# A hybrid decoder layer on one core: normalization in place, other buffers and another engine order at the four entries into a gated product

## The chip, the cores and the metric

The kernel runs on one core of a Trainium2 chip. The metric is the device time of one execution in microseconds, as the median of several runs. The engines are TensorE (PE; PEld is its weight load), VectorE (DVE), ScalarE (ACT), GpSimd (POOL) and SyncE (SP), whose queue issues most of the DMAs.

## The reference

One layer on x of 1024 tokens by 1024 features, all in fp32:

```python
x = x + 0.5 * swiglu(rms_norm(x, ffn1_norm), w_gate, w_up, w_down)       # D_FF = 2816
h = rms_norm(x, mix_norm)
fq, fk, fv, f_logit, sq, sk, sv, g_fox, g_sb = split_columns(h @ w_in)
...                                                                       # two attentions, 8 heads of 64 each
merged = sigmoid(g_fox) * (y_fox @ w_branch_fox) + sigmoid(g_sb) * (y_sb @ w_branch_sb)
x = x + merged @ w_out
x = x + 0.5 * swiglu(rms_norm(x, ffn2_norm), w_gate2, w_up2, w_down2)
x = x + sigmoid(rms_norm(x, ple_norm) @ w_ple_gate) * (p @ w_ple_proj)
```

`rms_norm` divides each token by the root of its mean square over the features and multiplies by a gain for each feature.

## The kernel before

x lies transposed: features on the 128 partitions, tokens along the row. `X[half]` holds 8 slices k of 128 features for one half of 512 tokens. Every fp32 operand is split in two parts that TensorE takes at its fast rate, a high part (a cast on ACT) and a low part (the fp32 value minus the high one); a product of two operands is three products, high by high, high by low and low by high. A "product" below is 12 matmuls of 128x128 by 128x512: four k and three combinations. An operand's split is `prep` for weights (`split`, L104 to L106, cast L105, subtraction L106) and `high` and `low` (L550 to L554) for activations.

The large matrix products use a block scheme with 7 products of sums and differences of blocks in place of 8. The activations of a gated product (`make_up`) are four quadrants (half of the tokens by half of the features) and the combinations that the scheme needs: `B[1]` and `B[2]` are half 0 (k 0 to 3 and 4 to 7), `B["12"]` and `B[3]` the same of half 1, `B[5]`, `B[6]`, `B[7]` and `B[4]` sums and differences. The weights' blocks are loaded by `load(n)` (two DMAs of 512 KB on SP's queue), summed by `sums(n)` and split by `prep(n, m)`; `product(n, m)` multiplies block m of column group n. The down products (`make_down`) work the same way, in chunks of 7 products, i from 0 to 6, each of four groups t of 12 matmuls (48 in all), with an eviction into X after each group (L442, L440).

There are four entries into a gated product: at the start (`first_entry`, ffn1), after ffn1's down pass (`mix_start`, the 6 column groups of the two mixer gates), after the output projection (`second_entry`, ffn2), and after ffn2's down pass (`ple_start`, 4 column groups). At an entry the half 0 of X is finished first, then half 1. For each half:

- `norm_sq` squares a slice on ACT (L189) and adds it up on GpSimd or VectorE (L191); `norm_sum` sums over the partitions with four tiny matmuls against a column of ones (L199), adds epsilon on VectorE (L201) and takes the power -0.5 on GpSimd (L202); `norm_row` transposes this into a row in PSUM, the same on all partitions (L208).
- `norm_mul` multiplies slice, gain and row on VectorE (L212) into slots of their own; `norm_high` and `norm_low` split half 0 into `B[1]` and `B[2]` (L217, L221); `combo_a` and `combo_b` do this for half 1 into `B["12"]` and `B[3]`.
- `plain(f, half)` is the direct product of column group 0 (f says which of its two blocks of 128 columns), 24 matmuls each (L482), whose result goes through the activation on ACT (`silu`, L490).
- `combo_t`, `combo_l`, `combo_u`, `combo_v`, `combo_s`, `combo_d` and `combo_e` make `B[5]`, `B[6]`, `B[7]` and `B[4]`. `combo_t` subtracts the high part of a quadrant of half 0 and then its low part (L590, L591), `combo_u` works on GpSimd (L598), `combo_v` on VectorE (L601), and `combo_d` subtracts and adds the two parts of `B[2]` (L611, L612).

At the mix, second and last entry this runs inside the last chunk of the down product before it: `up_begin` and `up_step` are called for each product i and group t, then `up_first` and `products`. After these comes the list of `up_order`, in which the product s is followed by its eviction, `begin(s)` and the preparation of product s + 4. At the start `first_entry` writes the order out by hand; there `busy` gives TensorE eight products of a zero tile with the slices of x as these arrive (L232).

Inside these parts each engine runs its instructions in the order in which the program issues them (`manual_schedule`), so an instruction that waits holds up all that are behind it on its engine. Buffers come from pools by tag (`BUFS`): a new tile of a tag waits until an older one of the same tag has been read for the last time.

In the last entry `finish` multiplies the gate with the projected embedding (`pd`), adds the residual (`xe`) and stores the result; for the groups n of 0 to 2 it does this on GpSimd (L1553, L1554), for n of 3 on VectorE, and `fetch` loads the two for later blocks.

Of the kernel before, what the change touches and what calls it, by code (L numbers as in the profile page):

```python
# [36 lines left out]
def tile_hybrid_decoder_layer(  # L37
# [131 lines left out]

    def norm_begin(X, i, tags):  # L170

        return {"x": X, "g": gains[:, i, :], "tags": tags, "s": {}}

    def norm_at(N, k):

        if "w" in N:
            i, j = k % 4, k // 4
            if i not in N["w"]:
                N["w"][i] = slot(N["tags"][i], [P, 2, 512])
            return N["w"][i][:, j, :]  # L180
        i, j = divmod(k, 2)
        if i not in N["s"]:
            N["s"][i] = slot(N["tags"][i], [P, 2, 512])
        return N["s"][i][:, j, :]

    def norm_sq(N, k, eng=nc.gpsimd):

        d = norm_at(N, k)
        nc.scalar.activation(d, N["x"][:, k, :], AF.Square, scale=D ** -0.5)  # L189
        if "acc" in N:  # L190
            eng.tensor_add(N["acc"], N["acc"], d)  # L191
        else:
            N["acc"] = d

    def norm_sum(N, ps):

        acc = N.pop("acc")
        for t in range(4):
            pe(nc.tensor.matmul(ps[:, t:t + 1], acc[:, t * P:(t + 1) * P], ones1[:], start=True, stop=True))  # L199
        rs = N["r"] = stat([P, 4], "rs")  # L200
        nc.vector.tensor_scalar(rs[:], ps[:, 0:4], EPS, None, ALU.add)  # L201
# [8 lines left out]

    def norm_mul(N, k):
        nc.vector.scalar_tensor_tensor(norm_at(N, k), N["x"][:, k, :], N["g"][:, k:k + 1], N["row"][:], ALU.mult, ALU.mult)  # L212

    def norm_high(N, k):
        if "B" not in N:
            N["B"] = [slot("H", [P, 2, 4, 512], F32R) for _ in range(2)]
        nc.scalar.copy(N["B"][k // 4][:, 0, k % 4, :], norm_at(N, k))  # L217

    def norm_low(N, k, eng=nc.vector):
        B = N["B"][k // 4]  # L220
        eng.tensor_sub(B[:, 1, k % 4, :], norm_at(N, k), f(B[:, 0, k % 4, :]))  # L221

    zero = []

    def busy(src=None):

        if src is None:
            zero.append(slot("T", [P, P]))
            nc.vector.memset(zero[0][:], 0.0)
            zero.append(bank("av"))  # L230
            return
        pe(nc.tensor.matmul(zero[1][:], zero[0][:], src, start=True, stop=True))  # L232
# [9 lines left out]
    def products(F):  # L242
# [3 lines left out]
        F.sums(1, nc.vector)  # L246
        F.b(3)
# [1404 lines left out]
```

## Time and profile before

| what | us |
|---|---|
| median of 3 runs | 2336.52 (2331.34 to 2337.04) |
| profiled execution | 2336.52 |
| its span | 2334.8 |
| TensorE busy | 2244.5 (96%) |
| VectorE busy | 1555.3 (67%) |
| ScalarE busy | 1003.1 (43%) |
| GpSimd busy | 911.6 (39%) |

In a row of a timeline stand the start, the duration, engine, line, operation, output and inputs, how many instructions were merged, and in brackets the idle time of the engine before it with what ended it. A row of the waits names who waited for whom, the sum, the number of times and the longest. A row of the windows gives the length of a stretch and each engine's busy time in it, then the clock granted to TensorE (1.00 is full), the share of DMA and its rate.

### The profile page before, as it was taken

The page shows a single profiled execution, that of the slowest core. Times are in us where ns is not written, and L with a number is a line of the kernel's source. Part 1 is how long each engine was busy: PE and PEld are TensorE (multiplying, and loading weights), DVE is VectorE, ACT ScalarE, POOL GpSimd, SP SyncE. Part 2 cuts the span into 40 slices and gives each one's busy share as a digit, 9 for nine tenths or more (in the row PEclk, how much of TensorE's full clock was granted, in tenths as well). Part 3 has the DMA queues.
Part 4 walks back from the last instruction along what each step waited for, and adds up shares of the span by engine and source line. Part 5 has one row for each costly group of instructions (what it writes and reads, how often), then busy time and mean ns, then how long its engine had stood idle before and what let it go on. Part 6 is the DMA issues. An engine that isn't in the chain of part 4 may idle for free.

```text
span 2334.8 us, 30467 instructions
## 1 busy us (share of the span) xinstructions
PE 2244.5 (96%) x11166; PEld 1888.5 (81%) x11166; DVE 1555.3 (67%) x2354; ACT 1003.1 (43%) x1782; POOL 911.6 (39%) x832
## 2 busy tenths in 40 slices
PE   6899999999998999999999999998999999999977
PEld 4688888888876899999898888876888888888755
DVE  5955555497879333656678785889554555878787
ACT  4433333343444435555566663344333333433433
POOL 3244344310032345566566664432544444100243
PEclk8999999999999999999999999999999999999999
DMA  3133232484331425333324367731423233852334
GB/s 127 56 107 127 77 126 82 158 303 157 130 102 55 147 78 159 100 91 84 89 56 100 109 190 233 255 125 33 135 91 113 99 105 112 298 195 100 126 116 163
DMA packets 197334, 298.04 MB, mean 128 GB/s; under 512 B 28984, under 2 KB 108856, under 8 KB 197184
## 3 DMA queue, kind: packets, MB, share of 16 engines
q1 hardware_dynamic: 196608, 296.08, 38.5%
q8 instruction: 88, 1.44, 0.3%
q14 instruction: 62, 0.51, 0.1%
q10 hardware_dynamic: 576, 0.02, 0.0%
HBM read 196.14 MB, written 83.13 MB: 120 GB/s over the span
## 4 chain that ended last, share of the span: by engine, by line
PE 78%; DVE 10%; issue 5%; ACT 3%; POOL 2%; DMA 1%; SPq 0%; POOLq 0%; DVEq 0%; ACTq 0%
PE ps L532 37%; PE ps L434 17%; PE ps L765 7%; PE ps L773 4%; PE ps L1368 3%; PE ps L1106 3%; PE ps L1080 2%; PE ps L1022 1%; PE ps L1021 1%; DVE H L106 1%; PE ps L927 1%; DVE PT L1088 1%; DVE RN L984 1%; DVE H L554 1%; DVE GF L984 1%
## 5 line engine op out<-in xcount | busy, mean ns | idle before, releaser
L434 PE MATMUL ps<-H,H 128*128 128x512 f32 x2184 | 499.2, 390 | 1.7 <-DVE X L442 1.2
L434 PEld LDWEIGHTS ps<-H,H 128*128 128x128 f32 x2184 | 410.1, 188 | 88.0 <-issue 2.9
L532 PE MATMUL ps<-H,WL 128*128 128x512 f32 x1164 | 280.3, 393 | 7.6 <-ACT WL L105 6.7
L532 PEld LDWEIGHTS ps<-H,WL 128*128 128x128 f32 x1164 | 220.4, 190 | 55.5 <-ACT WL L105 7.5
L532 PE MATMUL ps<-H,Q 128*128 128x512 f32 x648 | 154.8, 389 | 3.1 <-DVE Q L106 3.1
L532 PE MATMUL ps<-X,WL 128*128 128x512 f32 x600 | 145.9, 392 | 6.0 <-ACT WL L105 5.1
L532 PEld LDWEIGHTS ps<-H,Q 128*128 128x128 f32 x648 | 121.5, 188 | 28.8 <-DVE Q L106 3.6
L442 DVE SCALAR_TENSOR_TENSOR X<-ps,X 128x512 f32<-128x512 f32 x168 | 108.7, 683 | 53.9 <-PE ps L434 53.7
L532 PE MATMUL ps<-H,PT 128*128 128x512 f32 x516 | 132.0, 405 | 8.5 <-ACT H L551 5.0
L532 PEld LDWEIGHTS ps<-X,WL 128*128 128x128 f32 x600 | 113.3, 189 | 31.0 <-ACT WL L105 5.6
L532 PEld LDWEIGHTS ps<-H,PT 128*128 128x128 f32 x516 | 100.0, 196 | 35.1 <-ACT H L551 6.7
L191 POOL TENSOR_TENSOR WL<-WL 128x512 f32<-128x512 f32 x3 | 3.9, 1300 | 313.3 <-ACT WL L189 313.3
L139 POOL TENSOR_TENSOR WL<-RAW,WH 128x512 fp32r<-128x512 f32 (+1 forms) x84 | 98.5, 1194 | 68.4 <-ACT WH L129 44.0
L1088 DVE TENSOR_TENSOR PT<-ps,PT 128x512 fp32r<-128x512 f32 (+1 forms) x160 | 99.9, 627 | 30.2 <-ACT PT L1082 29.4
L765 PE MATMUL ps<-WH,H 128*128 128x256 f32 x768 | 116.1, 288 | 0.8 <-ACT RN L830 0.8
L773 PE MATMUL ps<-H,WH 128*128 128x512 f32 x384 | 115.0, 406 | 0.0
L1106 PE MATMUL ps<-PT,X 128*128 128x256 f32 (+1 forms) x640 | 102.6, 286 | 6.4 <-DVE PT L1088 5.5
L335 POOL TENSOR_TENSOR PT<-GF,RN 128x512 f32<-128x512 f32 x20 | 33.7, 1685 | 188.5 <-DVE GF L676 188.5
L1082 ACT CAST PT<-ps 128x512 fp32r<-128x512 f32 (+1 forms) x160 | 87.2, 549 | 42.5 <-PE ps L1080 41.2
L1106 PEld LDWEIGHTS ps<-PT,X 128*128 128x128 f32 x640 | 90.3, 190 | 17.0 <-DVE PT L1088 10.6
L765 PEld LDWEIGHTS ps<-WH,H 128*128 128x128 f32 x768 | 101.4, 190 | 2.6 <-ACT RN L830 1.3
L1034 POOL TENSOR_TENSOR T<-T,l 128x128 f32<-128x128 f32 (+3 forms) x64 | 73.2, 1148 | 72.2 <-DVE l L1033 70.1
(428 smaller groups left out, 4946.4 us busy)
## 6 DMA issues: line engine op xcount, KB each, us to landing
hidden<-PT SPq DMA_DIRECT2D x40, 512.0 KB, 3.1
WH<-in_ffn_w_gate_dram SPq DMA_DIRECT2D x38, 512.0 KB, 4.9
Q<-hidden SPq DMA_DIRECT2D x24, 512.0 KB, 6.5
hidden<-RN SPq DMA_DIRECT2D x22, 512.0 KB, 2.6
KH<-in_ffn_w_up_dram SPq DMA_DIRECT2D x20, 512.0 KB, 6.3
KL<-in_ffn_w_up_dram SPq DMA_DIRECT2D x20, 512.0 KB, 7.0
T<-in_ffn_w_down_dram SPq DMA_DIRECT2D x20, 512.0 KB, 5.9
GF<-hidden SPq DMA_DIRECT2D x14, 512.0 KB, 6.8
```

Of the source, the lines that this page charges most:

```text
L139: ins = eng_lo.tensor_sub(lo[part], raw[part], f(hi[part]))
L434: pe(nc.tensor.matmul(groups[g][t][:], wt[:, b, k, t * P:(t + 1) * P], act[:, a, k, :], start=(fresh and n == 0), stop=(i in (6, 1, 4) and ...
L442: nc.vector.scalar_tensor_tensor(xs, groups[g][t][:], scale, xs, ALU.mult, ALU.add)
L532: pe(nc.tensor.matmul(ps[:], hl[:, a, k, :], rhs(m, b, k), start=(first and i == 0), stop=(final and i == 11), skip_group_check=True))
L765: pe(nc.tensor.matmul(ps[:, :n], hT[t // 4](a, k)[:, (t % 4) * P:(t % 4 + 1) * P], w[k // 4][b][:, k % 4, :n], start=(i == 0), stop=(i == ...
L773: pe(nc.tensor.matmul(ps[:], w[a][:, k, :], hT[half](b, k), start=(i == 0), stop=(i == 23)))
L984: order("dve", nc.vector.tensor_tensor_scan(*args))
L1034: nc.gpsimd.tensor_mul(T[:, :n], T[:, :n], l[:].broadcast_to([P, n]))
L1082: high = nc.scalar.copy(pt[:, 0, :width], ps[:, :width])
L1088: ins = nc.vector.tensor_sub(pt[:, 1, :width], ps[:, :width], f(pt[:, 0, :width]))
L1106: pe(nc.tensor.matmul(o, lh, r, start=(kpair == c and i == 0), stop=(kpair == 0 and i == 3)))
L1368: pe(nc.tensor.matmul(ps[:], w[a][:, k, :], yT[g][b][:, k, half * 512:half * 512 + 512], start=(i == 0), stop=(i == 11)))
```

## The change

In words:

- `norm_mul` writes half 0 back into X, and later parts read the normalized fp32 value there (`norm_at`, `xk`). `combo_t` and `combo_d` become one subtraction each. `combo_u` and `combo_v` are one function on VectorE that also issues the cast of `B[6]`.
- The squares go through two halves of one scratch slot (`scratch`), with the running sum in another. Epsilon is added on ACT (`norm_pow`).
- At the three later entries the row of half 0 comes at group 2 of product 5, `load(0)` at product 4, `load(1)` at product 5 and `load(2)` after the last one; `prep(0, 1)` and `prep(0, 2)` stand at the end of product 4. The low parts of half 0 are all on VectorE. `prep(1, 1)`, `prep(1, 2)`, `sums(1)` stand ahead of the second row, and `combos` puts the first three low parts of `B["12"]` on GpSimd and the other five low parts of half 1 on VectorE.
- In `products` the differences and low parts of `B[5]` stand before `plain(0, 1)`, those of `B[6]` behind it; `up_order` begins with (2, 1), (1, 5), (2, 2), (1, 6).
- At the start `busy` is gone. The squares of half 0 are summed over the partitions slice by slice, with four tiny matmuls each that accumulate in PSUM. The two blocks of column group 0 take turns by k.
- In the last entry all `finish` work is on VectorE, put off until the next product's eviction has been issued (`lag`), and the last product is done in two halves of 256 columns.
- Tags of several operands change (`HOMES`, `UP_TAGS`, `tags_g`, `tags_p`); X's two slots are taken in the other order (`claim` writes one element to take the first).

The core of the diff:

```diff
+    def scratch():
+        return {"t": [slot("PT", [P, 2, 512]) for _ in range(2)], "n": 0}
...
+    def norm_sq(N, k, eng=nc.gpsimd, ps=None):
+        q = N["q"]
+        if ps is None and "acc" not in N:
+            d = N["acc"] = q["t"][0][:, N["half"], :]
+            nc.scalar.activation(d, N["x"][:, k, :], AF.Square, scale=D ** -0.5)
+            return
+        q["n"] += 1
+        d = q["t"][1][:, q["n"] % 2, :]
         nc.scalar.activation(d, N["x"][:, k, :], AF.Square, scale=D ** -0.5)
-        if "acc" in N:
+        if ps is None:
             eng.tensor_add(N["acc"], N["acc"], d)
-        else:
-            N["acc"] = d
+            return
+        for t in range(4):
+            pe(nc.tensor.matmul(ps[:, t:t + 1], d[:, t * P:(t + 1) * P], ones1[:], start=(k == 0 and t == 0), stop=(k == KD - 1), skip_group_check=True))
...
+    def norm_pow(N, ps):
         rs = N["r"] = stat([P, 4], "rs")
-        nc.vector.tensor_scalar(rs[:], ps[:, 0:4], EPS, None, ALU.add)
+        nc.scalar.activation(rs[:], ps[:, 0:4], AF.Copy, bias=EPS)
         nc.gpsimd.tensor_tensor(rs[:], rs[:], mhalf[:, 0:4], ALU.pow)
...
+    def norm_at(N, k):
+        if N["half"] == 0:
+            return N["x"][:, k, :]
+        i, j = k % 4, k // 4
+        if i not in N["w"]:
+            N["w"][i] = slot(N["tags"][i], [P, 2, 512])
+        return N["w"][i][:, j, :]
...
         ps = F.product(1, 2)
-        F.prep(1, 5)
+        F.t(0)
+        F.t(1)
+        F.l(0)
+        F.evict(1, 2, ps)
         F.prep(2, 1)
-        F.evict(1, 2, ps)
-        for k in range(4):
-            F.t(k)
-            if k:
-                F.l(k - 1)
-                F.u(k - 1, nc.gpsimd)
+        F.t(2)
+        F.l(1)
+        F.t(3)
+        F.l(2)
         F.l(3)
-        F.u(3, nc.gpsimd)
+        F.prep(2, 2)
         F.plain(0, 1)
         for k in range(4):
-            F.v(k)
-            F.s(k, 6)
-        F.prep(2, 2)
+            F.u(k)
+            if k:
+                F.s(k - 1, 6)
         F.plain(1, 1)
+        F.s(3, 6)
         F.prep(1, 6)
...
-        if i == 6:
+        if i == 4:
             F.load(0)
+        elif i == 5:
+            F.load(1)
...
     def up_first(N, F):
-        F.load(1)
-        F.prep(0, 2)
+        F.load(2)
         F.plain(0, 0, (0,))
         norm_sum(N[1], bank("sc"))
         F.prep(0, 5)
-        F.prep(0, 4, nc.gpsimd)
+        F.prep(0, 4)
+        F.prep(1, 1)
+        F.prep(1, 2)
+        F.sums(1, nc.vector)
         F.plain(0, 0, (1,))
         norm_row(N[1], bank("av"))
+        F.prep(1, 5)
+        F.plain(1, 0)
+        combos(F)
+        products(F)
+
+    def combos(F):
         F.a(0)
-        F.plain(1, 0, (0,))
+        F.b(0, nc.gpsimd)
         F.a(1)
-        F.b(0)
...
+        F.b(1, nc.gpsimd)
         F.a(2)
...
+        F.b(2, nc.gpsimd)
         F.a(3)
...
+        for k in range(3):
+            F.b(k)
+        F.b(3, nc.vector)
+        F.b(3)
...
-        seqn = [(1, 5), (2, 1), (1, 6), (2, 2), (1, 7), (2, 6), (2, 5), (1, 3), (2, 7), (1, 4)]
+        seqn = [(2, 1), (1, 5), (2, 2), (1, 6), (1, 7), (2, 6), (2, 5), (1, 3), (2, 7), (1, 4)]
...
-            d = t1(k)
-            nc.vector.tensor_sub(d, wk(k, 0), f(right(B[1], 0, k)))
-            nc.vector.tensor_sub(d, d, f(right(B[1], 1, k)))
-            high(5, k, d)
+            nc.vector.tensor_sub(xk(0, k), xk(1, k), xk(0, k))
+            high(5, k, xk(0, k))
...
         def combo_d(k):
-            nc.vector.tensor_sub(wk(k, 0), f(right(B[2], 0, k)), wk(k, 1))
-            nc.vector.tensor_add(wk(k, 0), wk(k, 0), f(right(B[2], 1, k)))
+            nc.vector.tensor_sub(xk(1, k), xk(0, k + 4), xk(1, k + 4))
...
         for k in range(KD):
-            norm_sq(N[0], k, nc.vector)
-            busy(X[0][:, k, :])
-        norm_sum(N[0], bank("pt"))
-        norm_row(N[0], bank("pf"))
+            norm_sq(N[0], k, ps=ps)
+        norm_pow(N[0], ps)
+        norm_row(N[0], bank("av"))
+        F.prep(0, 1)
+        F.prep(0, 5)
...
+            def work():
+                pt, xt = T[n, i]
+                nc.vector.tensor_mul(e[:, h, cols], e[:, h, cols], pt[:, h, cols])
+                nc.vector.tensor_add(e[:, h, cols], e[:, h, cols], xt[:, h, cols])
...
+            lag.append(work)
```

More of the change, by code (lines that the diff above doesn't have):

```diff
@@ L216, in norm_high, with claim @@
             N["B"] = [slot("H", [P, 2, 4, 512], F32R) for _ in range(2)]
-        nc.scalar.copy(N["B"][k // 4][:, 0, k % 4, :], norm_at(N, k))
+        nc.scalar.copy(N["B"][k // 4][:, 0, k % 4, :], N["x"][:, k, :])
     def norm_low(N, k, eng=nc.vector):
         B = N["B"][k // 4]
[L221 to L232, printed above, removed]
+        eng.tensor_sub(B[:, 1, k % 4, :], N["x"][:, k, :], f(B[:, 0, k % 4, :]))
+    def claim(t):
+        nc.vector.memset(t[:, 0, 0:1], 0.0)
     def finished(X, dst, half, k):
@@ L531, in product, with whole @@
                 for k in range(4):
-                    pe(nc.tensor.matmul(ps[:], hl[:, a, k, :], rhs(m, b, k), start=(first and i == 0), stop=(final and i == 11), skip_group_check=True))
+                    pe(nc.tensor.matmul(ps[:, cols], hl[:, a, k, :], B[m][b](k)[:, cols], start=(first and i == 0), stop=(final and i == 11), skip_group_check=True))
                     i += 1
             return ps
-        def rhs(m, b, k):
-            return right(B[m], b, k)
+        def whole(t):
+            return lambda k: t[:, 0, k, :], lambda k: t[:, 1, k, :]
         def home(m):
```

262 lines of the change are left out of this document (124 added, 138 removed).

## The prediction

> **What bounds the kernel now.** I read the page first, then busy time in windows around the four entries into a gated product (the start, and after each down pass or output projection), then TensorE's waits and the timeline there.
>
> ```profile
> span 2334.8 us, 30467 instructions
> ...
> PE 78%; DVE 10%; issue 5%; ACT 3%; POOL 2%; DMA 1%; SPq 0%; POOLq 0%; DVEq 0%; ACTq 0%
> ```
>
> The chain that ended last is TensorE for 78%; VectorE's 10% is where TensorE was held up. The windows show where (PE's x counts its matmul records, 24 small ones of the sums and rows in each entry):
>
> ```profile
> core 0: us, PE busy (x) PEld busy (x) DVE busy (x) ACT busy (x) POOL busy (x), PEclk, DMA share, GB/s
> 0.00:83.72 83.72, 57.23 (x185) 39.33 (x185) 52.39 (x75) 33.47 (x58) 25.86 (x27) 0.86 0.29 95
> 608.47:735.82 127.35, 116.84 (x504) 94.23 (x504) 102.48 (x124) 56.00 (x81) 36.10 (x25) 0.97 0.26 88
> 1486.46:1613.10 126.64, 115.66 (x505) 92.90 (x503) 109.38 (x134) 56.80 (x83) 37.13 (x25) 0.99 0.36 122
> 2137.86:2327.50 189.64, 168.08 (x708) 132.99 (x708) 149.41 (x177) 78.60 (x120) 66.86 (x38) 0.96 0.36 123
> ```
>
> Busy TensorE hides stretched matmuls, so I count. An undisturbed stretch gives the pace:
>
> ```profile
> 608.47 57.40 PE L434 MATMUL ps<-H,H 128*128 128x512 f32 x252 [0.61 <-DVE X L442]
> ...
> 735.82 4.39 PE L532 MATMUL ps<-T,WL 128*128 128x512 f32 x11 [3.39 <-ACT WL L105]
> ```
>
> 57.40/252 = 0.228 us each. By the code the windows hold 144, 480, 480 and 684 full matmuls; with about 3.8 us for sums and rows each (rows below), the work is 36.6, 113.1, 113.1 and 159.6 us. Lost: 47.1, 14.2, 13.5 and 30.0 us, some 105 us in all, and 7.3 us between the last matmul and the span's end. Elsewhere the up and down products run at the pace and the change leaves their order alone.
>
> What is lost in the mix entry:
>
> ```profile
> PE ps L532 <- ACT WL L105: 3.4, 1, 3.4
> PE ps L532 <- ACT Y L551: 2.5, 1, 2.5
> PE ps L208 <- POOL rs L202: 2.4, 1, 2.4
> PE ps L482 <- DVE H L554: 1.4, 1, 1.4
> ```
>
> ACT stands here as the releaser only because its casts follow VectorE's differences. VectorE is slow there because GpSimd works beside it:
>
> ```profile
> 714.88 0.69 DVE L590 TENSOR_TENSOR X<-Q,H 128x512 f32<-128x512 f32 x1
> 715.60 0.69 DVE L591 TENSOR_TENSOR X<-X,H 128x512 f32<-128x512 f32 x1
> 715.65 1.80 POOL L598 TENSOR_TENSOR Q<-Q 128x512 f32<-128x512 f32 x1 [4.36 <-DVE X L590]
> 716.21 1.78 DVE L590 TENSOR_TENSOR X<-Q,H 128x512 f32<-128x512 f32 x1
> ```
>
> The same VectorE difference takes 0.69 us alone and 1.78 us beside a GpSimd difference: 1.1 us a collision. An operation with one input in PSUM does not suffer:
>
> ```profile
> 683.78 1.55 POOL L191 TENSOR_TENSOR Q<-Q 128x512 f32<-128x512 f32 x1 [1.36 <-ACT Q L189]
> 685.00 0.69 DVE L442 SCALAR_TENSOR_TENSOR X<-ps,X 128x512 f32<-128x512 f32 x1 [0.83 <-PE ps L434]
> ```
>
> So norm_mul, whose row lies in PSUM, can run beside GpSimd.
>
> **Mix and second entry, part by part.** (1) Row of half 0. Epsilon moves from VectorE's queue to ACT's and the transposes move one group of 12 matmuls (2.7 us) later. That covers the whole 2.4 us wait; the multiplications start about where they did. (2) Gate weights load at products 4 and 5 and two are split in the down pass: two casts and two differences (2 x 0.69) go ahead of the last down operand on VectorE. TensorE still has three groups (8.2 us) to run then, so I cost it at nothing; without that cover it costs 1.4. On SP's queue load(0) passes the x_mid stores of products 4 to 6 and load(1) those of 5 and 6. Their buffers (GF, RN, WH) were released products earlier, so SP should not stop; if it did, the stores and the in-place multiplications behind them would be late. The in-place write adds a wait for those stores, which are issued a product earlier. (3) Squares go through two scratch halves in place of eight: each square waits for the sum two before it, 5.4 us back at one eviction per 2.7 us. Nothing. The new ACT epsilon of half 1 stops ACT until TensorE's sum; four gate casts queue behind it, but TensorE has 12 matmuls and a row (3.4 us) before it needs the first. Nothing, or up to 1.
>
> (4) From the second row on:
>
> ```profile
> 695.00 1.40 POOL L202 TENSOR_TENSOR rs<-rs,mhalf 128x4 f32<-128x4 f32 x1 [2.29 <-DVE rs L201]
> ...
> 698.05 2.72 DVE L212 SCALAR_TENSOR_TENSOR Q<-X,gains,ps 128x512 f32<-128x512 f32 x4 [2.53 <-PE ps L208]
> 698.83 2.60 ACT L551 CAST H<-Q 128x512 fp32r<-128x512 f32 x4 [0.62 <-DVE Q L212]
> ...
> 712.48 0.68 DVE L554 TENSOR_TENSOR H<-KH,H 128x512 fp32r<-128x512 f32 x1
> ```
>
> Now 15.1 us pass from row to last low part, with gate preparations and sums in between. After: one preparation, 8 multiplications (2.72/4 = 0.68) and 5 low parts on VectorE, 9.5 us, plus a collision or two with GpSimd's three remaining low parts. TensorE has 48 matmuls (10.9 us) to do meanwhile: the 1.4 us stall goes. Late next is ACT: its 8 casts (0.65) now queue behind the silu of the gate's half 0, 5.5 + 0.6 + 5.2 = 11.3 us, but the last isn't needed first.
>
> (5) Differences: t and d take one subtraction in place of two (8 fewer), while 4 u move from GpSimd, and four low parts and one preparation with them. The count on VectorE hardly changes; the collisions go. To B6's last low part it has 23 more operations, 15.3 us: 25.9 us after the row at the latest. TensorE reaches (1,6), with (2,2) now ahead of it, at 10.9 + 10.9 + 8.2 = 30.0. Slack of 4 us: stalls of 2.5 and 3.4 go, and the stretched matmuls between. (1,7) comes at 32.8, its operand at 31.2. prep(2,2) in front of plain(0,1) waits for a WL buffer that this very product frees; with VectorE's t and l still running then, it is covered.
>
> I leave 1.5 us of each entry's loss: gains of 12.7 and 12.0. Behind each entry the first 11 matmuls took 4.39 us, not 2.5, at the low clock that follows the 3.4 us stall: another 1.7, and the same behind the first entry, 5.1 in all.
>
> **First entry.**
>
> ```profile
> 4.22 9.71 PE L232 MATMUL ps<-X,T 128*128 128x512 f32 x16 [4.22 <-DMA X<-in_x_dram]
> 13.77 0.95 PE L199 MATMUL ps<-ones,PT 128*128 128x1 f32 x8
> 16.07 0.94 PE L208 MATMUL ps<-identf,rs 128*128 128x128 f32 x4 [1.36 <-POOL rs L202]
> 21.00 5.49 PE L482 MATMUL ps<-H,WL 128*128 128x512 f32 x12 [3.98 <-ACT WL L105]
> 27.94 1.19 PE L482 MATMUL ps<-H,WL 128*128 128x512 f32 x4 [1.45 <-ACT WL L105]
> 29.33 6.42 PE L482 MATMUL ps<-H,WL 128*128 128x512 f32 x20 [0.20 <-DVE WL L106]
> 40.51 1.87 PE L199 MATMUL ps<-ones,Q 128*128 128x1 f32 x8 [4.77 <-DVE Q L191]
> ```
>
> The eight filler products go, and 7 adds on VectorE. Instead each square gets its own four tiny products: 0.95 us at full clock, 1.87 after an idle spell. The sums start at 4.8 at the slow rate, as TensorE does now; I let that last some 5.5 us, as the slow stretch of 12 matmuls from 21.00 did, and then 0.95 each: they end near 14.6 and the row is there near 17.0, as now. No gain, no loss. The gain is behind it, where gate splits stand ahead of the multiplications, so that TensorE starts one multiplication and one cast after the row, at 18.4, not at 21.0. VectorE then: 4 multiplications to 19.7, 4 low parts with collisions to 23.5, 4 multiplications to 26.3, two preparations and 4 low parts to 31.5, the last two adds of the squares of half 1 to 33.9 (waiting for GpSimd's). The sum of half 1 ends at 35 (now 42.4); power, 12 matmuls and the row 38.4; one preparation 39.6, 8 multiplications 45.1, 5 low parts with collisions 49.3. TensorE has done (1,1) and (1,2) by 43.9 and waits in plain(0,1) for the fourth low part until 49.3; from there 12, 24 and 24 matmuls (13.7 us) make it 63.0 for the 144, in place of 83.7: 20.7 us. Its remaining waits are 5 us in plain(0,0) and 5 in plain(0,1), where VectorE is last.
>
> The rule against this: "TensorE: Matmul & The Clock Gate" of the Trainium skill, Part 1, says that the array falls to half rate after an idle window of about 3.4 us and needs about as long a busy stretch to recover, so fillers are worth keeping. The 12 matmuls at 21.00, after 4 us of idling, do show 0.46 us each, so the trace agrees on the fall. By that rule the tiny sums, back to back at half rate, would themselves warm the clock by 8.2 us: an estimate of half a microsecond better than my sum.
>
> **Gate at the end.** The same as the mix entry, then this:
>
> ```profile
> 474.75 1.23 DVE L676 TENSOR_TENSOR GF<-GF,Y 128x1024 f32<-128x1024 f32 x1 [0.53 <-ACT GF L667]
> ...
> 2254.16 4.52 DVE L554 TENSOR_TENSOR T<-X,T 128x512 fp32r<-128x512 f32 x2
> ```
>
> The finishing moves from GpSimd to VectorE: 12 operations of 1.23, 14.8 us, against collisions that cost 3 us in one pair of low parts. The first four (4.9) land ahead of B7: ready at 36.1 against 32.8, a stall of 3.3. Behind that VectorE has 38 us of work beside 43.7 of TensorE's. So 30.0 - 1.5 - 3.3 = 25.2 gained. The last product in column halves shortens the end from 7.3 to 4.7: 2.6. Reordered residual loads have 48 matmuls (10.9 us) before the first eviction wants them; claim is one tiny memset; both nothing.
>
> **Sum.** 20.7 + 12.7 + 12.0 + 25.2 + 2.6 + 5.1 = 78.3 us. This assumes that four in-order queues mesh. I take two residual stalls of the mix entry's typical 2.4 us per entry, 19 us: a gain of 59. The profiled execution took 2336.5 us (span 2334.8 and 1.7 around it), which is the median too. Forecast 2277 us, bounds 2258 (no residual) to 2290.
>
> **Rivals.** (a) Cold start: the tiny sums never warm the clock. Eight at 1.87 from 4.8 end at 19.8, the row at 22, then slow products: 8 us of the first gain lost, 2285. For: 40.51. Chance 0.13. (b) VectorE's order binds in part: preparations ahead of down operands and finishing ahead of B7 return most of it; 15 at the start, 3 in each middle entry, 8 and 2.6 at the end and nothing of the clock's 5.1 leave 2305 (2290 to 2328). Chance 0.15. (c) Slower: VectorE becomes the bound. All low parts of half 0 now sit there while GpSimd still adds up the squares: 7 collisions of 1.1 and one clock recovery, 9.4 us, in the last down products of three entries, and every eviction queues behind; plus 14.8 of finishing, against 20.7 + 2.6 gained: net 20 slower, 2356. It decides if VectorE's work in the last two down products exceeds TensorE's 96 matmuls (21.9 us). I count 25 operations of 0.68 (8 evictions, 8 multiplications, 8 low parts, 1 add), 17 us, and collisions that mostly fall on evictions from PSUM, which are immune. Chance 0.08. (d) No change: the gaps merely move, 2336. Against: four separate waits have four separate causes. Chance 0.04.
>
> **Numbers.** Forecast 0.60. The range 2258 to 2306 leaves out the slow half of (b), (c), (d): 0.19. Faster by over 0.3% (7 us, about what a measurement here can tell from none) 0.88, within it 0.04, slower 0.08.
>
> **What would show it.** Right: no TensorE wait for rs; VectorE differences at 0.69 between second row and (1,6); 144 matmuls done by 63 to 68 us; 480 in about 115 us. Wrong: granted clock near 0.5 through 20 to 40 us, evictions of the last down product queueing, or SP stopped at a gate load.

## The result and the profile after

The changed kernel takes **2272.16 us** (median of 4 runs, 2271.52 to 2273.09) against 2334.18 for the kernel before (4 runs, 2331.34 to 2337.04): a ratio of 0.9735, 95% interval 0.9718 to 0.9751. The forecast was 2277.0, the range 2258 to 2306. The profiled span is 2269.9 us, 64.9 less than before.

The page of the changed kernel, its busy times and its chain that ended last:

```profile
PE 2224.8 (98%) x11218; PEld 1888.9 (83%) x11218; DVE 1525.1 (67%) x2354; ACT 1000.0 (44%) x1791; POOL 832.1 (37%) x789
...
PE 84%; DVE 9%; ACT 2%; issue 2%; DMA 1%; POOL 0%; SPq 0%; DVEq 0%; ACTq 0%; POOLq 0%
```

TensorE's share of the chain rises from 78 to 84%; VectorE's falls only from 10 to 9%. The time went where the prediction looked for it. Windows from the same starts as before, the start of each last down chunk (or of the kernel), up to the start of a later product:

```profile
core 0: us, PE busy (x) PEld busy (x) DVE busy (x) ACT busy (x) POOL busy (x), PEclk, DMA share, GB/s
0.00:69.04 69.04, 56.76 (x224) 46.24 (x225) 41.87 (x67) 32.08 (x56) 14.72 (x20) 0.95 0.36 115
593.54:709.44 115.90, 115.11 (x516) 94.77 (x517) 100.64 (x128) 56.80 (x86) 25.20 (x17) 1.00 0.29 100
...
2094.64:2264.03 169.39, 160.73 (x720) 132.45 (x720) 145.00 (x186) 78.47 (x123) 25.15 (x18) 0.98 0.40 138
```

The first window holds the same 144 matmuls as before: the next one starts at 69.0 us (before 83.7, the last 3.3 of it a wait). The last one holds the same work, 684 matmuls (12 of them cut into two halves), in 169.4 us (before 189.6). The mix entry's window holds 492 matmuls here, one product more than before; the first 480 of them are through at 706.7, after 113.2 us (before 127.4, the last 3.4 a wait), which is the 113.1 us that the prediction counts for work alone. The table measures to the next point behind each entry that both kernels share (the end of the up pass, of the gate's products, of the second ffn's up pass, of the last matmul), so that slow matmuls behind a wait count as well:

| stage | gain forecast, with the clock's 1.7 behind it | gain measured |
|---|---|---|
| first entry | 22.4 | 14.9 |
| mix entry | 14.4 | 14.9 |
| second entry | 13.7 | 13.6 |
| last entry | 25.2 | 20.2 |
| tail behind the last matmul | 2.6 | 1.5 |
| sum | 78.3, less 19 for residual stalls: 59 | 65 |

What is left of TensorE's waits in the mix entry, in full:

```profile
PE ps L196 <- DVE PT L187: 0.8, 1, 0.8
PE ps L547 <- ACT GF L1192: 0.7, 1, 0.7
PE ps L447 <- DVE X L455: 0.6, 1, 0.6
```

The waits of 2.4 for the row, 1.4 and 2.5 for low and high parts and 3.4 for the operands behind them are all gone. The timeline shows by how little. First VectorE from the second row on, then TensorE at products (1, 6) and (1, 7):

```profile
679.49 0.69 DVE L510 TENSOR_TENSOR WH<-WH 128x512 f32<-128x512 f32 x1
...
688.90 3.94 DVE L568 TENSOR_TENSOR H<-KH,H 128x512 fp32r<-128x512 f32 x3
...
706.24 1.46 DVE L568 TENSOR_TENSOR T<-KH,T 128x512 fp32r<-128x512 f32 x2
708.01 0.69 DVE L106 TENSOR_TENSOR WL<-WH,WL 128x512 fp32r<-128x512 f32 x1 [0.31 <-ACT WL L105]
...
709.44 2.88 PE L547 MATMUL ps<-T,WL 128*128 128x512 f32 x12
713.00 1.20 PE L547 MATMUL ps<-T,WL 128*128 128x512 f32 x4 [0.68 <-ACT GF L1192]
```

The last low part of `B[6]` (L568) ends at 707.7 and the weights of (1, 6) at 708.7; TensorE takes them at 709.4. VectorE reaches this point from 682 with no idle time but the 0.31 us shown. Two things take longer there than the prediction has them: the row ends at 679.65, but VectorE is still in the sums of column group 1 (L510 and the two operations behind it) until 681.6, and the three low parts at 688.90 take 1.31 us each and not 0.69, with GpSimd in its own three until 691.7.

The first entry, TensorE:

```profile
5.33 13.81 PE L190 MATMUL ps<-ones,PT 128*128 128x1 f32 x64 [5.33 <-ACT PT L185]
20.51 1.11 PE L208 MATMUL ps<-identf,rs 128*128 128x128 f32 x4 [1.36 <-POOL rs L202]
23.11 10.24 PE L495 MATMUL ps<-H,WL 128*128 128x512 f32 x32 [1.49 <-ACT H L226]
```

The tiny sums show as 64 records, eight for each slice. They take 13.8 us, 0.216 each, and the row is there at 21.6. And the largest wait that is left, in the last entry, with the engines that hand it on:

```profile
2209.33 1.22 DVE L1559 TENSOR_TENSOR GF<-GF,Y 128x1024 f32<-128x1024 f32 x1
...
2211.89 0.36 SPq L1561 DMA_DIRECT2D out_dram<-GF  x1
...
2215.00 0.58 ACT L1583 COPY GF<-ps 128x512 f32<-128x512 f32 x1 [6.31 <-DMA out_dram<-GF]
...
2219.12 0.58 ACT L1585 COPY GF<-ps 128x512 f32<-128x512 f32 x1
...
2219.75 4.37 PE L547 MATMUL ps<-H,WL 128*128 128x512 f32 x12 [6.76 <-ACT GF L1585]
```

Product (1, 7) accumulates in the PSUM bank of (1, 6) and waits 6.76 us for that eviction (L1585). It stands on ScalarE behind the eviction of (2, 1) (L1583), which stops ScalarE for 6.31 us: it writes into the buffer GF of column group 0, which comes free when its finishing on VectorE (L1559, L1560) and its store are done.

### The profile page after: what moved, and what is told of

Its sections match the earlier page's. It is cut to its first block, busy times and chain, and to the rows that moved or that the text cites. A ratio compares the mean times of both kernels' runs of the same rounds, so it can differ in the third digit from the quotient of the medians.

```text
span 2269.9 us, 30559 instructions
## 1 busy us (share of the span) xinstructions
PE 2224.8 (98%) x11218; PEld 1888.9 (83%) x11218; DVE 1525.1 (67%) x2354; ACT 1000.0 (44%) x1791; POOL 832.1 (37%) x789
## 4 chain that ended last, share of the span: by engine, by line
PE 84%; DVE 9%; ACT 2%; issue 2%; DMA 1%; POOL 0%; SPq 0%; DVEq 0%; ACTq 0%; POOLq 0%
PE ps L547 39%; PE ps L447 18%; PE ps L770 7%; PE ps L778 5%; PE ps L1373 4%; PE ps L1111 3%; PE ps L495 2%; PE ps L1085 2%; PE ps L1027 1%; PE ps L1026 1%; DVE H L106 1%; PE ps L932 1%; DVE H L230 1%; DVE PT L1093 1%; DVE X L221 1%
## 5 line engine op out<-in xcount | busy, mean ns | idle before, releaser
L547 PE MATMUL ps<-H,WL 128*128 128x512 f32 x1152 | 273.5, 391 | 6.9 <-ACT GF L1585 6.8
L187 POOL TENSOR_TENSOR PT<-PT,PT 128x512 f32<-128x512 f32 x41 | 55.3, 1348 | 425.2 <-ACT PT L185 424.1
L547 PE MATMUL ps<-X,WL 128*128 128x512 f32 (+1 forms) x588 | 138.7, 385 | 0.6 <-ACT RN L1611 0.6
L1111 PEld LDWEIGHTS ps<-PT,X 128*128 128x128 f32 x640 | 90.3, 190 | 16.7 <-DVE PT L1093 10.3
```

The source lines that it names most:

```text
L547: pe(nc.tensor.matmul(ps[:, cols], hl[:, a, k, :], B[m][b](k)[:, cols], start=(first and i == 0), stop=(final and i == 11), skip_group_che ...
L1111: pe(nc.tensor.matmul(o, lh, r, start=(kpair == c and i == 0), stop=(kpair == 0 and i == 3)))
```

## The experiments

Two theories stand against each other: (1) collisions with GpSimd and four separate waits were the loss, as the prediction has it; (2) VectorE's amount and order of work is what TensorE waits for; and for the two places that missed the forecast, a cold clock at the start and the release of a buffer, or VectorE's work, in the last entry. Each ratio is to the kernel before, run beside it; the kernel after has 0.9735. The stages are those of the table above, read from one profiled execution each.

### The first finishing at once (e1_finish_now)

```diff
-            lag.append(work)
+            if (n, i) == (0, 0):
+                work()
+            else:
+                lag.append(work)
```

> The changed kernel with one edit: in the last entry the finish work of block (0, 0) is issued at once, right after its gate, and not put off until the eviction of (2, 1). Theory 1 (buffer): the 6.76 us wait of TensorE at (1, 7) is ScalarE held at the eviction of (2, 1), whose GF buffer is free only when the store of block (0, 0) has gone out; then the wait falls to under 1.5 us, the slow matmuls behind it (4.37 us for 12) fall to about 3.0, and the time falls by 5 to 8 us against the changed kernel, to about 2265. Theory 2 (VectorE's order, as the prediction had it: the finish work stands ahead of B7's low parts): the four operations still stand ahead of B7 on VectorE, the wait keeps at least 3 us and the time falls by no more than 3.

Measured: 2271.85 us, ratio 0.9733 (0.9715 to 0.975): no gain. TensorE's waits in the last entry:

```profile
PE ps L547 <- ACT GF L1588: 3.8, 1, 3.8
PE ps L547 <- DVE RN L1591: 1.5, 1, 1.5
PE ps L547 <- ACT WL L105: 0.9, 1, 0.9
```

The buffer's release did hold the eviction: it comes 4 us earlier, and 6.8 becomes 3.8. But the finishing now stands ahead of the low parts of `B[6]` on VectorE, and a new wait of 0.9 appears at (1, 6); at the end 1.5 in place of 0.6. The entry is 0.2 us shorter. The buffer alone is not the cause.

### Filler ahead of the tiny sums (e2_prefill)

```diff
+        zt = slot("T", [P, 2, 512])
+        nc.vector.memset(zt[:, 0, :], 0.0)
+        zb = bank("pf")
+        for _ in range(3):
+            pe(nc.tensor.matmul(zb[:], zt[:, 0, 0:P], zt[:, 0, :], start=True, stop=True))
```

> The changed kernel with one addition: at the very start TensorE multiplies a zero tile by itself three times (128x512, fp32), before x arrives; nothing reads the product. In the changed kernel the 64 records of the tiny sums took 13.81 us, 0.216 each, the slow rate from first to last. Theory 1 (the fill warms the clock, and the tiny sums keep it): records at 0.12, the sums end near 13 instead of 19.1, the first entry's 144 matmuls end 5 to 7 us earlier and the time is about 2266. Theory 2 (tiny sums do not count as work for the clock): the first few groups run at 0.12 and the rest at 0.216 again; the sums end between 15 and 18, a gain of 1 to 4 us. Theory 3 (the rate of these sums has nothing to do with the clock): 0.216 throughout, no gain or 1 us lost.

Measured: 2271.99 us, ratio 0.9732 (0.9712 to 0.9751). TensorE:

```profile
1.58 4.42 PE L1409 MATMUL ps<-T 128*128 128x512 f32 x6 [1.58 <-DVE X L234]
6.02 1.95 PE L190 MATMUL ps<-ones,PT 128*128 128x1 f32 x16
8.42 10.40 PE L190 MATMUL ps<-ones,PT 128*128 128x1 f32 x48 [0.45 <-ACT PT L185]
```

The filler warms the clock: the next 16 tiny records take 0.122 us each. Then they fall back to 0.217 and stay there. The row is only 0.3 us earlier, the 144 matmuls end 1.75 earlier, and the median shows nothing of it. So it isn't only that the sums start cold: these one-column matmuls do not keep the clock up.

### The squares of half 0 added up on VectorE (e7_vector_sums)

```diff
-        ps = bank("sc")
-        for k in range(KD):
-            norm_sq(N[0], k, ps=ps)
-        norm_pow(N[0], ps)
+        for k in range(KD):
+            norm_sq(N[0], k, nc.vector)
+        norm_sum(N[0], bank("sc"))
```

> The changed kernel with the sum of half 0 in the first entry made as in the kernel before: squares added up on VectorE (0.69 us each), then one group of tiny sums; without the filler products. Theory 1 (the tiny sums at the slow rate set the first row): the sums end near 14.4 and the row comes near 16.5 instead of 21.6; the 144 matmuls of the first entry end 4 to 5 us earlier, about 2267. Theory 2 (something later in the entry, VectorE's queue or the second half's sum, sets its end): the row comes earlier but the end moves by less than 2 us.

Measured: 2269.37 us, ratio 0.9718 (0.9701 to 0.9735), 2.8 us below the kernel after by the medians. The profiled execution is the fastest of the four, 4.8 us shorter than that of the kernel after.

```profile
13.12 1.87 PE L196 MATMUL ps<-ones,PT 128*128 128x1 f32 x8 [13.12 <-DVE PT L187]
16.35 1.11 PE L208 MATMUL ps<-identf,rs 128*128 128x128 f32 x4 [1.36 <-POOL rs L202]
...
64.61 3.56 PE L547 MATMUL ps<-H,WL 128*128 128x512 f32 x15
```

The row is there at 17.5 and the 144 matmuls are done at 64.6, 4.4 us sooner. The tiny sums, which replaced seven adds on VectorE, cost some 4 us here: two later runs that differ by this edit alone (e9 and e10) lie 4.25 us apart by their medians.

### GpSimd's work put back (e3_gpsimd_back)

The kernel after, in its own order, with the first half of each u, two low parts of half 0, four of `B[3]`, one preparation and the finishing of groups 0 to 2 on GpSimd again; the three low parts of `B["12"]` come back to VectorE. One of the places:

```diff
-            nc.vector.tensor_sub(xk(1, k), xk(1, k + 4), xk(1, k))
+            nc.gpsimd.tensor_sub(xk(1, k), xk(1, k + 4), xk(1, k))
```

> The changed kernel with only the placement on GpSimd undone: the first subtraction of u, all four low parts of B3, low parts 4 and 5 of half 0 (5 and 7 at the start), the preparation (0, 4) and the finish work of groups 0 to 2 go back to GpSimd; order, in-place normalization, single differences, early gate weights stay. Theory 1 (collisions between GpSimd and VectorE made the stalls): 1.1 us per collision, 6 to 9 collisions per middle entry against 4 us of slack, so 3 to 5 us come back in each of the two middle entries, 3 to 5 at the start and 5 to 10 at the end: 14 to 25 us slower than the changed kernel, 2286 to 2297. Theory 2 (the order and the early preparations made the gain, the slack now covers collisions): less than 6 us comes back, under 2278.

Measured: 2288.86 us, ratio 0.9803 (0.9786 to 0.9819), 16.7 us slower than after. By stage: 1.9 at the start, 2.7 in the mix entry, 1.9 in the second, 7.1 in the last, 3.4 in the tail. The collisions are there as before:

```profile
692.10 3.48 DVE L562 TENSOR_TENSOR H<-KH,H 128x512 fp32r<-128x512 f32 x2
695.50 2.38 DVE L585 TENSOR_TENSOR X<-Q,X 128x512 f32<-128x512 f32 x2
```

1.74 and 1.19 us each in place of 0.69. Yet in a middle entry VectorE is only some 1.3 us later at the last low part of `B[6]` (29.3 us behind the row in place of 28.05), since GpSimd also takes a net five operations off it there (four u and four low parts go, three come back). GpSimd's absence is worth 2.7 us of the 14.9 in the mix entry and 1.9 of the 13.6 in the second.

### The kernel before with a later row (e4_row_later)

```diff
-        nc.vector.tensor_scalar(rs[:], ps[:, 0:4], EPS, None, ALU.add)
+        nc.scalar.activation(rs[:], ps[:, 0:4], AF.Copy, bias=EPS)
...
-            elif t == 1:
+            elif t == 2:
                 norm_row(N[0], bank("pf"))
-            for k in ((), (0, 1), (2, 3, 4), (5, 6, 7))[t]:
+            for k in ((), (), (0, 1, 2, 3), (4, 5, 6))[t]:
```

> The kernel before, with only the row of half 0 moved: epsilon on ACT, transposes and the first multiplications one group of 12 matmuls later, at the three later entries (and epsilon on ACT at the start). Theory 1 (waits with separate causes add up): the 2.4 us wait for rs goes at each of three entries, and nothing of it comes back: 7 to 8 us faster than before, so near 2328. Theory 2 (the later waits for operands absorb it, since VectorE's work from the second row on sets when the operands of (1,5) and (1,6) are there): the wait goes and the later ones grow by as much, 0 to 2 us faster. The trace of it shows which: the waits of the mix entry were 2.4 for rs, then 1.4, 2.5 and 3.4.

Measured: 2328.33 us against 2335.81, ratio 0.997 (0.996 to 0.998): 7.5 us, the sum that the first theory had. Waits in the mix entry:

```profile
PE ps L534 <- ACT Y L553: 2.5, 1, 2.5
PE ps L534 <- ACT WL L105: 2.4, 1, 2.4
PE ps L484 <- DVE H L556: 1.4, 1, 1.4
```

The wait for the row is gone; the last of the others has even shrunk, from 3.4 to 2.4. In the second entry it has grown, from 3.4 to 3.9:

```profile
PE ps L534 <- ACT WL L105: 3.9, 1, 3.9
```

In both the wait for the sums of half 1 has grown from 0.5 to 1.0. So by stage the gain is uneven: 3.7 us in the mix entry, 2.8 in the last, 1.2 in the second, where the second theory holds in part.

### The kernel before without GpSimd's work (e5_gpsimd_off_alone)

```diff
-                F.u(k - 1, nc.gpsimd)
+                F.u(k - 1)
...
-                norm_low(N[0], k, nc.gpsimd if k in (4, 5) else nc.vector)
+                norm_low(N[0], k)
...
-        def finish(n, i, e, hs=slice(0, 2), eng=nc.gpsimd, more=True):
+        def finish(n, i, e, hs=slice(0, 2), eng=nc.vector, more=True):
```

> The kernel before, with only GpSimd's SBUF work at the entries moved to VectorE (the four u, four low parts of B3, two low parts of half 0, one preparation, and all finishing of the last entry), in the old order and with the two subtractions. Theory 1 (collisions are the cost, 1.1 us each): some 7 collisions, 7.7 us, against 11 moved operations of 0.68, 7.5 us, an entry: little in sum, but the collisions sat on the critical differences, so 1 to 3 us faster an entry; the finishing adds up to 14.8 us of VectorE in the last entry, 3 to 5 of it on the path: 0 to 8 us faster in all. Theory 2 (VectorE's amount of work is what TensorE waits for, and the new order is what pays): every moved operation is late work: 0 to 15 us slower. Putting GpSimd's work back into the new kernel cost 16.7 us, so if this run is not faster, the two parts need each other.

Measured: 2322.49 us, ratio 0.9949 (0.9934 to 0.9964), 13.3 us faster, more than either theory gave. By stage: 2.6 at the start, 1.4 in the mix entry, 0.5 lost in the second, 9.4 in the last. The shown lines are three of the places; the low parts of `B[3]` and a preparation move as well. The mix entry shows the trade, by its waits:

```profile
PE ps L532 <- ACT WL L105: 5.2, 1, 5.2
PE ps L208 <- POOL rs L202: 2.4, 1, 2.4
PE ps L532 <- ACT Y L551: 1.4, 1, 1.4
```

The waits of 2.5 and 1.4 shrink to 1.4 and 0.2, and the one for the operands behind them grows from 3.4 to 5.2: what no longer collides is now extra work on VectorE. In the last entry, where the finishing moved too, the change of engine alone was worth 9.4 us, though 14.8 us of work went to VectorE.

### The second subtraction paid again (e6_two_differences)

```diff
+        def again(d):
+            nc.vector.tensor_sub(d, d, zero1[:, 0:1].broadcast_to([P, 512]))
...
             nc.vector.tensor_sub(xk(0, k), xk(1, k), xk(0, k))
+            again(xk(0, k))
...
             nc.vector.tensor_sub(xk(1, k), xk(0, k + 4), xk(1, k + 4))
+            again(xk(1, k))
```

> The kernel after, with the second subtraction of each difference in t and d paid again (a subtraction of a column of zeros in place, 8 operations of about 0.68 us an entry; the result does not change). Theory 1 (VectorE has some 4 us of slack between the second row and (1,6), as the prediction has it): 0 to 2 us slower at each entry, 2 to 6 in all, most of it in the last one, where TensorE waits already. Theory 2 (the single differences are what makes the order fit): four of the eight stand ahead of (1,6), 2.7 us, and the other four ahead of (1,4), so 2.7 to 5.4 us slower an entry, 10 to 20 in all.

Measured: 2298.27 us, ratio 0.9843 (0.9828 to 0.9858): **26 us slower than after**, more than the second theory's 10 to 20. By stage: 7.5 at the start, 5.2 in the mix entry, 8.1 in the second, 4.5 in the last. VectorE, and TensorE's waits in the mix entry:

```profile
700.58 0.69 DVE L590 TENSOR_TENSOR X<-X,zero 128x512 f32<-128x512 f32 x1
```

```profile
PE ps L549 <- DVE WL L106: 1.9, 1, 1.9
PE ps L549 <- ACT GF L1199: 1.6, 1, 1.6
PE ps L549 <- ACT WL L105: 1.3, 1, 1.3
```

Eight operations of 0.69 us are 5.5 us an entry, 22 in all, and they cost 25 at the four entries: on the whole TensorE pays for them in full, and in the mix entry it waits four times behind (2, 2), 1.3, 1.6, 1.9 and 0.6 us, where it waited 0.7 once. So in the kernel after the middle entries hang on the amount of VectorE's work. What its new order gained is not shown by this run.

### (1, 6) and (1, 7) no longer neighbours (e8_apart)

```diff
-        seqn = [(2, 1), (1, 5), (2, 2), (1, 6), (1, 7), (2, 6), (2, 5), (1, 3), (2, 7), (1, 4)]
+        seqn = [(2, 1), (1, 5), (1, 6), (2, 2), (1, 7), (2, 6), (2, 5), (1, 3), (2, 7), (1, 4)]
```

> The kernel after, with (1,6) and (2,2) exchanged in the order of products, so that (1,6) and (1,7), which use the same PSUM bank, are no longer neighbours and the eviction between them has 2.7 us more. Theory 1 (TensorE waits there for that eviction): the 0.7 us wait at (1,7) goes in the mix and second entry and the 6.8 us one in the last entry falls by 2.7, 4 us faster in all. Theory 2 (VectorE's low parts of B6 are the limit, ready only 1.7 us ahead of their use): (1,6) now comes 2.7 us earlier and waits 1 us at each entry, so nothing is gained in the middle, and 1 to 2 us in the last entry.

Measured: 2273.25 us, ratio 0.9739 (0.9724 to 0.9753): nothing gained. Waits in the last entry:

```profile
PE ps L547 <- ACT GF L1585: 4.8, 1, 4.8
PE ps L547 <- ACT WL L105: 1.2, 1, 1.2
```

6.8 becomes 4.8, but (1, 6), asked for one product earlier, now waits 1.2 us for its weights, in the middle entries too, where the wait of 0.7 at (1, 7) goes. The second theory holds: `B[6]` and its weights have less than a product of slack.

### The second finishing late (e9_second_finish_late)

```diff
+            elif (n, i) == (0, 1):
+                late.append(work)
...
+            if (n, m) == (2, 6):
+                lag[:0] = late
+                late.clear()
```

> The kernel after, with the first finishing of the last entry (0, 0) done at once, as in the run that did so for it alone, and the second (0, 1) put off to the eviction of (2, 6). In that earlier run the eviction of (2, 1) came 4 us sooner and the 6.8 us wait at (1, 7) fell to 3.8, while 0.9 and 1.0 us of new waits took the rest back; ScalarE then waited 2.1 us for a sum of weights on VectorE that stands behind the second finishing (2.45 us of VectorE). Theory 1 (VectorE has no slack between the second row and (1, 7), so each of its operations there is paid in full, and slack behind 2227): the wait falls to about 1.5 and the last entry shortens by 2 to 4 us. Theory 2 (the release of the buffer of E[0] is the cause by itself): no change against that run, 0 to 0.5 us.

Measured: 2270.49 us, ratio 0.9726 (0.9713 to 0.9739). Waits in the last entry:

```profile
PE ps L547 <- ACT GF L1593: 2.7, 2, 1.6
PE ps L547 <- DVE RN L1596: 2.4, 1, 2.4
PE ps L547 <- ACT WL L105: 0.9, 1, 0.9
```

At (1, 7) the wait is down to 1.6, as expected: release and VectorE's work together made the 6.8. But the entry is only 0.9 us shorter (168.45 in place of 169.39): 2.4 and 1.1 us came back near the end.

### Both repairs (e10_sums_and_finish), and filler (e11_and_filler)

The first run joins the edits of e7 and e9. The second adds to it, at the start:

```diff
+        zt = slot("T", [P, P])
+        nc.vector.memset(zt[:], 0.0)
+        zb = bank("pf")
         for k in range(KD):
             norm_sq(N[0], k, nc.vector)
+            if k < 7:
+                pe(nc.tensor.matmul(zb[:], zt[:], X[0][:, k, :], start=True, stop=True))
```

> The kernel after, with the squares of half 0 at the start added up on VectorE in the manner of before (that alone took the span from 2269.9 to 2265.1), and the finishing of the run beside this one. If the two add up: 2 to 4 us below 2269.4, so 2265 to 2268. If the last entry gains nothing: 2269.

> The run beside this one, and in addition seven products of a zero tile with the slices of x while these arrive, the kind that the kernel before had, to hold TensorE's clock up until the sums. Theory 1 (behind the row VectorE's low parts set the pace of plain(0, 0), as its waits of 0.9 and 1.2 us for them show): the tiny sums take 0.95 instead of 1.87, the row comes 0.9 us sooner, and the 32 matmuls at 0.32 us each become 0.23, but then wait for VectorE: 1 us faster. Theory 2 (the slow clock is what the first entry loses): 0.9 + 32 x 0.09 = 3.9 us faster.

Measured: 2266.24 us, ratio 0.971 (0.9697 to 0.9724), and 2266.13, ratio 0.9707 (0.9694 to 0.972). The filler is worth nothing: it halves the eight records of the sum (0.95 in place of 1.87), but the 32 matmuls behind the row still take 10.56 us, since the clock falls again in the 3.5 us between the sum and these. The first run's last entry still loses time near its end, and SyncE's queue and VectorE show to what:

```profile
2232.10 0.34 SPq L1560 DMA_DIRECT2D out_dram<-GF  x1
2237.81 0.32 SPq L1552 DMA_DIRECT2D Y<-p_proj  x1
...
2242.40 1.23 DVE L1558 TENSOR_TENSOR RN<-RN,Y 128x1024 f32<-128x1024 f32 x1 [1.55 <-DMA Y<-p_proj]
```

Block (1, 0) is finished at 2232 and frees the pair of buffers T, but the next loads in the list are for the pair Y, which block (1, 1) frees only at 2237.8. SyncE stands in between, the loads land late, and VectorE waits for them in six places, 5.5 us, with evictions and preparations queued behind.

### The loads sooner (e12_loads_sooner)

```diff
-                tag = "KH" if (n, i) == (2, 0) else ("Y", "T")[len(T) % 2]
+                tag = {(2, 0): "KH", (2, 1): "T", (3, 0): "Q"}.get((n, i), ("Y", "T")[len(T) % 2])
...
-                    if (n, i) == (2, 1):
+                    if n == 1:
                         fetch()
```

> The run with VectorE's sums and the late second finishing, and in addition other buffers for the residual loads of the last entry: the loads of block (2, 1) take the pair that (1, 0) frees in place of the pair that (1, 1) frees 7 us later, those of (3, 0) take the pair Q, which nothing uses any more there, and both pairs are asked for one finishing earlier. In that run SyncE's queue stood from 2232.4 to 2237.8 in front of the load of Y, VectorE then waited 5.5 us in six places for p_proj and x_end, and TensorE lost 1.1, 2.8 and 1.5 us (slow matmuls after the wait) behind it. Theory 1 (what the two earlier repairs of the last entry gained at (1, 7) was given back because the end of the entry hangs on these loads): the waits for the loads go and the end comes 3 to 5 us sooner, 2261 to 2263. Theory 2 (the end is VectorE's and ScalarE's amount of work): the waits for loads go, others take their place, 0 to 1 us, 2265 to 2266.

Measured: **2261.58 us**, ratio 0.968 (0.9665 to 0.9696), the fastest version, 10.6 us below the kernel after and 4.7 below the run with both repairs. VectorE:

```profile
2240.65 1.22 DVE L1558 TENSOR_TENSOR RN<-RN,T 128x1024 f32<-128x1024 f32 x1
2241.90 1.23 DVE L1559 TENSOR_TENSOR RN<-RN,T 128x1024 f32<-128x1024 f32 x1
```

No wait for a load is left on VectorE, TensorE's wait of 2.8 us is gone, and the last entry takes 165.4 us (169.4 in the kernel after).

## Why the prediction was right, and where its steps were off

**Middle entries: gains right, slack wrong.** 14.9 and 13.6 us against 14.4 and 13.7. The term for the row is confirmed in sum (7.5 us in e4, where the prediction had 2.4 at each of three entries), though not entry by entry. But of the 4 us of slack that step 5 gave to (1, 6), 0.74 was there: the last low part came 28.05 us behind the row, not 25.9, and the weights of (1, 6) another 1.0 behind it, which the step did not count. The 2 us arose in step 4: its 9.5 us from the row to the last low part of half 1, with one or two collisions, were 13.2, because 2.0 us of the sums of column group 1 still ran behind the row and the three low parts beside GpSimd's took 1.9 longer. The 23 operations behind them took 14.9, where the step had 15.3. VectorE paces these entries to within a microsecond, and e6 shows that the eight saved subtractions were not a small term: 26 us of the kernel's time hang on them. The prediction counted them against the four u that came from GpSimd and held that the count hardly changes and the collisions go; the runs turn the weight round. GpSimd's absence is worth 2.7 and 1.9 us in the two middle entries (e3; 1.4 and -0.5 in e5), the later row 1.2 to 3.7 (e4), the single differences 5 to 8 (e6). In the mix entry these are 2.7, 3.7 and 5.2 of 14.9, if they may be added, with two taken from the kernel after and one from the kernel before; the rest, the order of products and of preparations and the first weights in the down pass, was not tried by itself and stays open. Over the whole kernel the three come to some 50 of the 62 us (26, 16.7 and 7.5), with the same reserve.

**First entry: rival (a) held.** The sums were to warm up within 5.5 us and end near 14.6 (15.1 by the step's own terms: 5.5 us at 1.87 a group, the rest at 0.95); they ended at 19.1 and the row came at 21.6 (rival: 19.8 and 22). The entry fell 7.5 us short of its forecast, and the rival had 8. The 144 matmuls were done at 69.0, not 63.0. The rival's total of 2285 did not come, only because the allowance below covered the loss. The rule of the page "TensorE: Matmul & The Clock Gate" of the Trainium skill, Part 1, by which back-to-back sums would themselves warm the clock, did not hold for them: 13.8 us of them stayed slow, and in e2 they fell back from a warm start. The rest of the step was good: with the row at 17.5 (e7; forecast 17.0) the 144 end at 64.6 (63.0).

**Last entry: the term for the finishing was mis-sized and had a second part.** The stall at `B[7]` was put at 3.3 us, from 4.9 us of finishing on VectorE; it was 6.8, and 1.5 more in the 12 slow matmuls behind it (4.37 us in place of the 2.88 that 12 take elsewhere). That work counts (e9: 2.2 us of the wait), but the step missed that the eviction of (2, 1) needs the buffer that this finishing releases, and that ScalarE holds the eviction of (1, 6) behind it (e1: 3 us). It also took the work behind it, 38 us beside 43.7, as covered. In amount it is; but the loads that `fetch` makes for the finishing reach VectorE late, because their buffers are asked for in an order other than the one in which they come free. The prediction has no term for these loads; the reordered ones that it costs at nothing are those that the evictions into X want. e12 prices the late loads at 4.7 us once the earlier stall is gone. In the kernel after, the stall ahead of them hid part of that: when the stall was cut (e9), the last waits grew from 0.6 to 2.4 and 1.1.

**Tail.** 7.3 became 5.85, not 4.7. TensorE ends at 2264.0, and VectorE has block (2, 0) ahead of the last halves:

```profile
2261.56 1.23 DVE L1559 TENSOR_TENSOR GF<-GF,KH 128x1024 f32<-128x1024 f32 x1 [0.21 <-DMA KH<-p_proj]
2262.82 1.22 DVE L1560 TENSOR_TENSOR GF<-GF,KH 128x1024 f32<-128x1024 f32 x1
```

Six more operations follow these, to 2267.0. That work, too, stood behind the late loads, but these explain only half of the miss: with the loads sooner (e12) the tail is still 5.3 us.

**The allowance.** 19 us were taken off for two residual stalls of 2.4 us per entry. The middle entries had one of 0.7 each. What the allowance paid for was 7.5 at the start, 5.0 in the last entry and 1.1 in the tail, none of which it was made for, so the forecast came out 5 us too slow. That the total was nearer than its terms is luck.

**Rival (c)** had the right engine and the wrong place: VectorE is without slack, but between the second row and (1, 7), not in the last down products, where TensorE waits 0.6 us at their start and 0.8 for a sum. **Rival (b)** had its mechanism in the last entry alone.

## What to carry to other kernels

When the waits of an entry disappear, look at how much idle time is left on the engine that feeds it before calling anything slack: paying one saved cost again (e6) told more here than undoing GpSimd's part (e3). Of moved work ask not only how long it takes, but which buffer its end releases, which engine is stopped by that, and in which order an in-order queue asks for buffers against the order in which they come free. A repair that does not shorten a stage may still be right, with a second limit close behind: the late finishing gained 1.7 us by itself (e9), and the loads asked for sooner another 4.7 behind it (e12).

## What the runs showed of the hardware that was not expected

One-column matmuls did not warm TensorE. In the kernel after, 64 records in a row took 0.216 us each for 13.8 us. In e2, behind 4.42 us of 512-column filler, 16 of them took 0.122 each, and then they fell back to 0.217, with a gap of no more than 0.45 us between. The 512-column matmuls behind the row did warm it. The windows of e2 show both, with the granted clock behind the busy times:

```profile
8.42:18.80 10.38, 10.38 (x48) 10.31 (x48) 0.00 (x0) 3.15 (x5) 0.00 (x0) 0.50 1.06 379
22.79:28.70 5.91, 5.91 (x12) 3.99 (x13) 5.91 (x10) 4.49 (x9) 2.78 (x2) 0.50 0.23 79
28.70:33.30 4.60, 4.60 (x21) 3.57 (x19) 2.81 (x4) 3.74 (x8) 2.81 (x3) 1.00 0.00 1
```

All through the one-column sums the clock stood at 0.50; after 5.9 us of wide matmuls, 0.49 us each, it was back at 1.00, and the next took 0.23 each. In the kernel after, the windows of the first 33 us show a granted clock of 1.00 although the sums ran at the slow rate. The trace has no entry for the clock before 27.9 us there, so the durations are the evidence up to that point.

The eight records of a sum are as good as the clock that they find, 0.95 or 1.87 us, but warming it for them alone brought nothing (e11): it fell again in the 3.5 us up to the next work.
